# Attention scores from stacked queries and two stacked key parts: two 512-column matmuls a head and block, context keys laid first

## The chip, the core and the metric

The kernel runs on one core of a Trainium2 chip. The metric is the device time of one execution in microseconds (us); lower is better. The engines are named as in the profile: PE is TensorE's matmul stream, PEld its weight loads, DVE is VectorE, ACT ScalarE, POOL GpSimd, and SP the engine whose queue issues the DMAs.

## The reference

Two layers of a block with 512 latent tokens and 256 context tokens, each layer an input projection to three groups of heads, an output projection and a gated feed-forward. The change lies in one of the three groups, neighbourhood attention with six heads of 64 features. Its scores are

```python
s_loc = jnp.einsum('bhrqd,bhrakd->bhrqak', qg, kb) * scale + bias
s_loc = jnp.where(col_ok[:, None, :], s_loc, -jnp.inf)
s_ctx = jnp.einsum('bhrqd,bnhd->bhrqn', qg, kc) * scale
s = jnp.concatenate([s_loc.reshape(B, H, R, GRID_W, n_loc), s_ctx], axis=-1)
p = jax.nn.softmax(s, axis=-1)
o = local probabilities @ vb + context probabilities @ vc
```

A latent query sees a window of latent keys with a learned bias, and all 256 context keys, in one softmax. In the first layer the context tokens also attend to themselves; in the second layer only latent queries are left.

## The kernel before

Every float32 operand is held as two float32r parts, high and low, and a product is the sum of high by high, low by high and high by low in PSUM. So most of the kernel is `mm3` (three matmuls).

The attention takes the heads in three pairs (`Heads(pr)`, pr = 0 to 2), and a pair in blocks of 128 queries: b = 0 to 2 are three columns of the latent grid, each with 256 latent keys of its window; b = 3 collects the two borders, whose 256 keys are the first and the last tile of the latent keys; b = 4, in the first layer only, is the 256 context queries against the 256 context keys. A latent block has 512 scores a query, 256 local and 256 of the context. One head and block fill one PSUM bank, tag `a`, of which there are three.

`features_of_heads` transposes queries and keys of a pair to feature-major tiles `qt` and `kt` ([128, 2, columns]: the two heads on partitions 0 to 63 and 64 to 127, the two parts in the middle). `stack` then copies by DMA: per head a tile `st` with both parts of the queries on 128 partitions, and one with the high part of the keys twice, so that a single matmul over 128 partitions gives (high q + low q) by high k. The remaining product, high q by low k, is a matmul over 64 partitions straight from `qt` and `kt`. `product` emits this: two matmuls for 256 scores, four a head for a latent block. Pair 0 has no stacks in its first two blocks and uses `mm3` over 64 partitions, six matmuls a head.

The order on PE is written by hand (`manual_schedule`); the other engines' queues come from a scheduler. For unit n of (pair, block), PE does

1. the scores of unit n, both heads;
2. the eight transposes of unit n-1's probabilities `p` into two banks of tag `b`;
3. a filling of about 2.3 us of the output projection of the other branches (`wo`: rows `m<-u,whl`, each weight tile from a DMA `raw<-in_woa` and split by ACT and DVE into `whl`);
4. one step of the next pair's `features_of_heads` (`next(pairs[pr + 1].prepare)`);
5. the values of unit n-1 (`y<-pT,vn`), for which ACT and DVE have copied the transposes to `pT`.

Between 1 and 2 of the next unit lies the softmax: DVE adds the bias and takes the maximum (`s`, `mx`), POOL negates it (`nm`), ACT exponentiates (`p`), DVE divides (`rcl`, `p`).

`qt` and `kt` of an odd pair are in another pool than those of an even one, so the tiles of two pairs exist side by side. Each stack has two buffers.

Of the kernel before, what the change touches and what calls it, by code (L numbers as in the profile page):

```python
"""Two layers of the FNet / neighbourhood attention / GLA block with a context prefix, on one core.

The residual streams stay feature-major on chip. Dense products run on the tensor engine with
both operands split exactly into two float32r parts (x = hi + lo); the three products that count
at float32 accuracy are accumulated in PSUM.
"""
# [28 lines left out]
# ------------------------------------------------------------------ host: layout and constants  # L35
# [43 lines left out]
def _rpb_index():  # L79
    """Per tile variant: index of the bias for (query in tile, key in window), -1 where masked."""  # L80
# [60 lines left out]
# ------------------------------------------------------------------ the kernel  # L141

def hybrid_kernel(tc, d, out, dbg=None):
# [55 lines left out]
    # ---- constants  # L199
# [12 lines left out]
    # ---- residual streams  # L212
# [12 lines left out]
    # ---- conditioning vectors  # L225
# [14 lines left out]
    # ---- work that is emitted some units of dense work after what it depends on  # L240
# [18 lines left out]
    def ada_steps(l, qs, rawp, bufs, PS, nk=4, pool_streams=(1,), on_pe=()):  # L259
        """Modulation of layer l, in steps of one weight chunk; each step loads the next chunk first.  # L260

        The products are added over the feature tiles elementwise, and over the partitions by the tensor engine.
        """
# [65 lines left out]
    def ada_first(n, rawp, bufs):  # L329
        """The first layer's shift and scale (of the first norm) for one tile of features, in two steps."""  # L330
# [25 lines left out]
    def norm_add(acc, x, k, tp, e):  # L356
        """Adds the squares of one group of features."""
        if k == 0:
            act(acc, x, AF.Square)
            return  # L360
        sq = mk(tp, [128, TL], F32, "nsq", 2)[:, :x.shape[-1]]
        act(sq, x, AF.Square)
        tt(e, acc, acc, sq, ALU.add)

    def norm_acc(xs, n, tp, e):
        """Squares summed over the features of a partition."""
        acc = mk(tp, [128, TL], F32, "nacc", 2)[:, :n]
        for k in range(KD):
            norm_add(acc, xs[k], k, tp, e)
        return acc, n  # L370
# [4 lines left out]
    def norm_sums(parts, tp, more=None):  # L375
        """1 / rms of each token, with the tokens on the partitions."""
# [13 lines left out]
    def norm_spread(sums, tp):  # L390
        """1 / rms of each token (column), on every partition, in PSUM."""
# [8 lines left out]
    def norm_mod(items, tp):  # L400
        """h = rms_norm(x) * sc + sh for groups of features, written as two float32r parts.

        Without rb the columns of x are normalised already.
        """
# [26 lines left out]
    def wload(p, src, shape, rb=2, hb=2, cap=None, tag="whl", e=V):  # L431
        """A weight chunk from DRAM, as its two float32r parts."""
# [11 lines left out]
    for l in range(DEPTH):  # L444
# [6 lines left out]
        # ================= input projection, with the chunk states of the linear attention  # L451
# [27 lines left out]
        def first_projection():  # L479
            """The first column group of the first layer, as its modulation arrives by feature tiles."""  # L480
# [75 lines left out]
        def group(src, cols, specs, evac, together=0, w=None, ps=None, after=None):  # L556
            """Token-major products of one column group; specs lists (tile, first column).

            The last `together` tiles are accumulated side by side, as their operands arrive.
            """  # L560
# [63 lines left out]
        # gates, decays and the state that each chunk of 64 tokens adds, per direction  # L624
# [103 lines left out]
        def open_outputs():  # L728
            """Takes the place of the tiles of the steps above, and runs the states through the chunks."""
# [69 lines left out]
        def between():  # L799
            """After each tile of the last groups: the outputs of the linear attention, a tile at a time."""  # L800
# [13 lines left out]
        # Fourier branch, feature-major  # L814
# [38 lines left out]
        # ================= gated linear attention: outputs  # L853
# [31 lines left out]
        def stack(p, pr, t, is_q):  # L885
            """Per head both parts of the queries on 128 partitions, or the high part of the keys twice."""
            n = t.shape[-1]
            for hh in range(2):
                u = stacks[pr, hh, is_q] = mk(p, [128, n], F32R, f"st{hh}{int(is_q)}", 2)
                for part in range(2):  # L890
                    nc.sync.dma_start(out=u[64 * part:64 * part + 64].bitcast(F32),
                                      in_=t[64 * hh:64 * hh + 64, part * is_q].bitcast(F32))

        def features_of_heads(p, pr, out, sp=None):
            """Queries and keys of two heads, feature-major, as two float32r parts, in steps."""
# [4 lines left out]
            for src, dst, gain in ((kn, kt, None), (qn, qt, qg)):  # L900
                for (j0, nj) in ((0, 4), (4, 2)):
                    if src is qn and j0 and not ctx_q:
                        continue
                    sl = slice(128 * j0, 128 * (j0 + nj))
# [14 lines left out]
        def wout(src, nk, streams, kinds, whole=False, split_at=KD, begin=0):  # L919
            """Adds the projection of nk feature tiles.  # L920

            From output tile split_at on, one stream is finished before the next; with `whole` all weights stay.
            All but the last feature tile of the first `begin` output tiles of the first stream are added at once.
            """
# [43 lines left out]
        def to_features(i):  # L968
            """The heads' outputs of one tile of tokens, feature-major, as two float32r parts."""
# [7 lines left out]
        # Fourier mixing  # L977
# [5 lines left out]
        def fourier():  # L983
# [9 lines left out]
            def features(t, parts, rows):  # L993
                """The 64-point transforms and the linear map, of up to 128 (folded) positions."""
# [66 lines left out]
        def load_bias(p, h):  # L1061
            bias[h] = bi = mk(p, [128, 3, 256], F32, "bias", 2)
            nc.sync.dma_start(out=bi[:, 0:2], in_=d["rpb"][l, h])
# [339 lines left out]
```

## Time and profile before

| | |
|---|---|
| time, median of 3 runs | 1725.89 us (1725.5 to 1730.17) |
| profiled execution, first to last instruction | 1724.6 us |
| PE busy | 1680.6 us (97%), 9992 matmuls |
| DVE, ACT, POOL busy | 926.9, 584.2, 239.9 us |
| attention units, first layer | about 302 to 418 us of the span |
| attention units, second layer | about 1240 to 1334 us |
| mean granted clock of TensorE | 0.989 of full speed |

The profiled execution has no time of its own beside its span; the span lies 1.3 us below the median of the runs, and sums below are made against the span. Busy time of PE contains the modelled tail of each matmul and overlaps the weight loads, so 97% does not say that nothing could be shorter: what a group of matmuls costs is the distance from its first start to the start of what follows.

### The profile page before, as it was taken

To read this page: it belongs to the slowest core of one execution; us is meant where nothing else is said; L and a number is where in the kernel's file an instruction comes from. 1 tells how busy PE (TensorE), PEld (TensorE's weight loads), DVE (VectorE), ACT (ScalarE), POOL (GpSimd) and SP (SyncE) were. 2 spreads that over 40 slices of the span, in tenths; PEclk is the share of its full clock that TensorE was granted. 3 is DMA by queue.
4 is the path that set the end of the run, shared out by engine and by line. 5 is a ranking of instruction groups with operands and counts; after the bars stand their busy time and mean duration, and the time that the engine had idled before them with its cause. 6 is when DMAs were issued, how large, how long until landed. Compare 5 with 4: busy or idle time off the path is not lost.

```text
span 1724.6 us, 25165 instructions
## 1 busy us (share of the span) xinstructions
PE 1680.6 (97%) x9992; PEld 1433.0 (83%) x9992; DVE 926.9 (54%) x1649; ACT 584.2 (34%) x1027; POOL 239.9 (14%) x280
## 2 busy tenths in 40 slices
PE   6999999999899999999999999999899899999999
PEld 5888898777788888888888889899777888888887
DVE  6799765665855544544533434453566744344332
ACT  4474224444343422221122323831444432222220
POOL 0242331002222210000000011332100400000000
PEclk9999999899899999999999999999999999999999
DMA  9555435622233343433411311222643233323321
GB/s 323 170 163 166 157 96 167 187 57 81 75 110 111 122 147 110 137 124 106 147 62 55 122 37 38 83 88 65 190 134 93 76 122 98 98 90 93 102 86 58
DMA packets 79474, 195.94 MB, mean 114 GB/s; under 512 B 10296, under 2 KB 26492, under 8 KB 78332
## 3 DMA queue, kind: packets, MB, share of 16 engines
q1 hardware_dynamic: 79356, 194.34, 36.1%
q8 instruction: 78, 1.28, 0.3%
q14 instruction: 40, 0.33, 0.1%
HBM read 172.81 MB, written 12.85 MB: 108 GB/s over the span
## 4 chain that ended last, share of the span: by engine, by line
PE 90%; DMA 3%; DVE 2%; ACT 2%; issue 1%; SPq 0%; POOL 0%; DVEq 0%; ACTq 0%
PE a L179 32%; PE m L179 25%; PE b L179 21%; PE y L179 11%; PE b L1168 2%; DMA raw<-in_woa 1%; DVE u L190 1%; DVE whl L187 1%; DVE nacc L187 0%; DMA u<-xs 0%; DMA bias<-in_rpb 0%; ACT whl L193 0%; DMA adaw<-in_ada 0%; ACT ab L193 0%; DMA qn<-scr_q 0%
## 5 line engine op out<-in xcount | busy, mean ns | idle before, releaser
L193 ACT ACTIVATE whl<-raw 128x1024 fp32r<-128x1024 f32 (+7 forms) x222 | 204.9, 927 | 396.5 <-PE a L179 142.7
L187 DVE TENSOR_TENSOR whl<-raw,whl 128x1024 fp32r<-128x1024 f32 (+7 forms) x201 | 222.6, 1110 | 86.0 <-ACT whl L193 85.6
L179 PE MATMUL m<-u,whl 128*128 128x512 f32 (+1 forms) x1278 | 266.1, 360 | 0.4 <-DVE whl L187 0.4
L179 PE MATMUL a<-u,whl 128*128 128x512 f32 (+1 forms) x1299 | 248.1, 347 | 3.1 <-ACT u L193 2.4
L179 PEld LDWEIGHTS m<-u,whl 128*128 128x128 f32 x1278 | 213.7, 193 | 34.1 <-issue 1.2
L179 PEld LDWEIGHTS a<-u,whl 128*128 128x128 f32 x1299 | 210.0, 190 | 34.7 <-ACT u L193 2.8
L179 PE MATMUL b<-u,whl 128*128 128x512 f32 (+1 forms) x915 | 184.7, 352 | 3.7 <-DVE whl L187 2.1
L179 PEld LDWEIGHTS b<-u,whl 128*128 128x128 f32 x915 | 151.7, 192 | 28.9 <-DVE whl L187 2.6
L190 DVE SCALAR_TENSOR_TENSOR adac<-adaw,u,adac 128x512 f32<-128x512 f32 x196 | 157.4, 826 | 23.0 <-DMA adaw<-in_adaw 21.6
L179 PE MATMUL b<-whl,u 128*128 128x384 f32 (+1 forms) x696 | 143.9, 343 | 1.6 <-DVE u L190 0.9
L179 PE MATMUL m<-whl,u 128*128 128x384 f32 (+2 forms) x672 | 138.7, 343 | 0.9 <-ACT u L193 0.9
L179 PEld LDWEIGHTS b<-whl,u 128*128 128x128 f32 x696 | 121.8, 188 | 8.8 <-issue 4.7
L179 PE MATMUL a<-g,whl 128*128 128x512 f32 (+1 forms) x594 | 126.7, 370 | 0.0
L179 PEld LDWEIGHTS m<-whl,u 128*128 128x128 f32 x672 | 115.7, 188 | 11.8 <-issue 7.8
L179 PEld LDWEIGHTS a<-g,whl 128*128 128x128 f32 x594 | 103.9, 189 | 19.4 <-DVE adac L293 0.8
L190 DVE SCALAR_TENSOR_TENSOR ft<-ft,a 128x512 f32<-128x512 f32 (+1 forms) x53 | 30.5, 576 | 111.6 <-ACT ft L193 77.1
L179 PE MATMUL y<-u,whl 128*128 128x512 f32 (+1 forms) x420 | 82.5, 349 | 0.1
L179 PEld LDWEIGHTS y<-u,whl 128*128 128x128 f32 x420 | 68.1, 189 | 12.1 <-issue 0.8
L179 PE MATMUL m<-g,whl 128*128 128x512 f32 (+1 forms) x396 | 77.8, 350 | 0.0
L187 POOL TENSOR_TENSOR nacc<-nacc,nsq 128x256 f32<-128x256 f32 (+1 forms) x21 | 20.5, 975 | 395.1 <-ACT nsq L193 394.8
L179 PEld LDWEIGHTS m<-g,whl 128*128 128x128 f32 x396 | 64.7, 189 | 9.7
L179 PE MATMUL b<-g,whl 128*128 128x256 f32 (+1 forms) x396 | 72.6, 336 | 0.0
(207 smaller groups left out, 2082.2 us busy)
## 6 DMA issues: line engine op xcount, KB each, us to landing
raw<-in_w SPq DMA_DIRECT2D x104, 512.0 KB
adaw<-in_adaw SPq DMA_DIRECT2D x48, 512.0 KB
adaw<-in_adaw SPq DMA_DIRECT2D x64, 256.0 KB
raw<-in_wg SPq DMA_DIRECT2D x40, 384.0 KB
raw<-in_w SPq DMA_DIRECT2D x32, 448.0 KB
adaw<-in_ada SPq DMA_DIRECT2D x8, 1024.0 KB
raw<-in_woa SPq DMA_DIRECT2D x16, 320.0 KB
st<-kt SPq DMA_DIRECT2D x24, 192.0 KB
```

Of the source, the lines that this page charges most:

```text
L179: T.matmul(o, lhsT=l, rhs=r, start=start, stop=stop, skip_group_check=True)
L187: e.tensor_tensor(out=o, in0=a, in1=b, op=op)
L190: V.scalar_tensor_tensor(out=o, in0=a, scalar=s, in1=b, op0=op0, op1=op1)
L193: S.activation(out=o, in_=i, func=f, **kw)
L1168: T.transpose(ps[:, 128 * j:128 * j + 128], p[:, 128 * j:128 * j + 128], ident)
```

## The change

Keys are laid with the 256 context columns first. The low part of the keys is stacked twice as well (`stack` now makes kinds 0 and 1 of the keys and 2 of the queries), so the second product also runs over 128 partitions and adds low by low. A block's local and context keys are addressed as one operand of 512 columns. `products` emits per head two matmuls of 512 columns for b = 0 to 2; for b = 3 two of 384 and two of 128; for b = 4 four of 256. Pair 0's first two blocks keep 64 partitions, with three matmuls of 512 columns a head, the two heads in turns. The `qt` and `kt` of all pairs share one buffer, so the steps of the next pair wait for block 1: no step at b = 0, two at b = 1. The bias tile and the order of the value products follow the new layout of the keys.

```diff
         def stack(p, pr, t, is_q):
             n = t.shape[-1]
             for hh in range(2):
-                u = stacks[pr, hh, is_q] = mk(p, [128, n], F32R, f"st{hh}{int(is_q)}", 2)
-                for part in range(2):
-                    nc.sync.dma_start(out=u[64 * part:64 * part + 64].bitcast(F32),
-                                      in_=t[64 * hh:64 * hh + 64, part * is_q].bitcast(F32))
+                for kind in ((2,) if is_q else (0, 1)):
+                    u = stacks[pr, hh, kind] = mk(p, [128, n], F32R, f"st{hh}{kind}", 2)
+                    for part in range(2):
+                        nc.sync.dma_start(out=u[64 * part:64 * part + 64].bitcast(F32),
+                                          in_=t[64 * hh:64 * hh + 64, part if is_q else kind].bitcast(F32))
...
-                    sl = slice(128 * j0, 128 * (j0 + nj))
+                    c0 = 128 * j0 if src is qn else (128 * j0 + 256) % 768
+                    sl = slice(c0, c0 + 128 * nj)
...
-            nc.sync.dma_start(out=bi[:, 0:2], in_=d["rpb"][l, h])
-            G.memset(bi[:, 2], 0.0)
+            nc.sync.dma_start(out=bi[:, 1:3], in_=d["rpb"][l, h])
+            G.memset(bi[:, 0], 0.0)
...
-                    self.prepare = features_of_heads(own, pr, feats, np_)
+                    self.prepare = features_of_heads(nap, pr, feats, np_)
...
-            def product(self, b, o, hh, q0, k, start, stop):
-                r, q = slice(64 * hh, 64 * hh + 64), slice(q0, q0 + 128)
+            def products(self, b, parts):
                 qt, kt = feats[self.pr]
+                sps = [PA() for _ in self.hds]
                 if self.pr or b >= 2:
-                    mm(o, stacks[self.pr, hh, True][:, q], k(stacks[self.pr, hh, False]), start, False)
-                    mm(o, qt[r, 0, q], k(kt[r, 1]), False, stop)
+                    for hh, sp in enumerate(sps):
+                        st_ = [stacks[self.pr, hh, i] for i in range(3)]
+                        for n, (o, q0, k) in enumerate(parts):
+                            for i in range(2):
+                                mm(o(sp), st_[2][:, q0:q0 + 128], k(st_[i]), n == i == 0, i == 1)
+                    return sps
+                for n, (o, q0, k) in enumerate(parts):
+                    for i, j in ((0, 0), (1, 0), (0, 1)):
+                        for hh, sp in enumerate(sps):
+                            r = slice(64 * hh, 64 * hh + 64)
+                            mm(o(sp), qt[r, i, q0:q0 + 128], k(kt[r, j]), n == i == j == 0, j == 1)
+                return sps
...
+            def scores(self, b):
+                if b == 4:
+                    parts = [(lambda a, t=t: a[:, 256 * t:256 * t + 256], 512 + 128 * t, lambda k: k[:, 0:256])
+                             for t in range(2)]
+                elif b == 3:
+                    parts = [(lambda a: a[:, 0:384], 384, lambda k: k[:, 0:384]),
+                             (lambda a: a[:, 384:512], 384, lambda k: k[:, 640:768])]
                 else:
-                    mm3(o, qt[r, 0, q], qt[r, 1, q], k(kt[r, 0]), k(kt[r, 1]), start, stop)
+                    cut = ((512, 256, 1), (768, 384, 1), (768, 256, 2))[b]
+                    pair = lambda k: k[:, :cut[0]].rearrange("p (a b) -> p a b", b=cut[1])[:, ::cut[2], 0:256]
+                    parts = [(lambda a: a.rearrange("p (a b) -> p a b", a=2), 128 * b, pair)]
...
                 if pr < 2 and n < len(units):
-                    next(pairs[pr + 1].prepare, None)
+                    for _ in range((0, 2, 1, 1, 1)[b]):
+                        next(pairs[pr + 1].prepare, None)
```

On PE, at pair 0, block 2 of the first layer, the first unit that uses stacks (`st` tiles; `a` is the bank of a head), there stood before

```order
L179 MATMUL a_3550<-st_691_3392,st_693_3398 128x256
L179 MATMUL a_3550<-kt_3123,qt_3122 128x256
L179 MATMUL a_3550<-st_691_3392,st_693_3398 128x256
L179 MATMUL a_3550<-kt_3123,qt_3122 128x256
L179 MATMUL a_3566<-st_692_3395,st_694_3401 128x256
L179 MATMUL a_3566<-kt_3123,qt_3122 128x256
L179 MATMUL a_3566<-st_692_3395,st_694_3401 128x256
L179 MATMUL a_3566<-kt_3123,qt_3122 128x256
```

and now, between the same values of the unit before and the same transposes, stand

```order
L179 MATMUL a_3544<-st_691_3392,st_695_3404 128x512
L179 MATMUL a_3544<-st_692_3395,st_695_3404 128x512
L179 MATMUL a_3545<-st_693_3398,st_696_3407 128x512
L179 MATMUL a_3545<-st_694_3401,st_696_3407 128x512
```

The eight matmuls that took 128 and 64 partitions in turns are four over 128 partitions.

On SP's queue, at the start of the first layer's attention, between the loads of the residual and the bias of pair 1, there stood before (x2: one DMA for each half of the partitions)

```order
L419 DMA raw_3673<-in_woa 128x640
L891 DMA st_691_3392<-kt_3123 64x768 x2
L891 DMA st_692_3395<-kt_3123 64x768 x2
L891 DMA st_693_3398<-qt_3122 64x768 x2
L891 DMA st_694_3401<-qt_3122 64x768 x2
L1063 DMA bias_3442<-in_rpb 128x512
```

and now

```order
L419 DMA raw_3669<-in_woa 128x640
L892 DMA st_691_3392<-kt_3123 64x768 x2
L892 DMA st_692_3395<-kt_3123 64x768 x2
L892 DMA st_693_3398<-kt_3123 64x768 x2
L892 DMA st_694_3401<-kt_3123 64x768 x2
L892 DMA st_695_3404<-qt_3122 64x768 x2
L892 DMA st_696_3407<-qt_3122 64x768 x2
L1065 DMA bias_3442<-in_rpb 128x512
```

Four more DMAs stand ahead of those of the queries, and of all that follows. It is the same at the start of the second layer's attention, where two biases and the next weight tile `raw_11718<-in_woa` follow, and at each later pair.

On ACT, at the start of the second layer's attention, the split of that weight tile stood before both the rest of the keys and the softmax of block 2:

```order
L193 ACTIVATE p_11735,sml_11736<-s_11731,nm_11733 128x512
L193 ACTIVATE whl_11757<-raw_11755 128x640
L193 ACTIVATE kt_11697<-b_11773 128x256
L193 ACTIVATE p_11797,sml_11798<-s_11793,nm_11795 128x512
L193 ACTIVATE pT_11831<-b_11826 128x512
```

Now there stands

```order
L193 ACTIVATE p_11698,sml_11699<-s_11694,nm_11696 128x512
L193 ACTIVATE kt_11737<-b_11738 128x512
L193 ACTIVATE kt_11737<-b_11745 128x256
L193 ACTIVATE whl_11720<-raw_11718 128x640
L193 ACTIVATE p_11770,sml_11771<-s_11766,nm_11768 128x512
```

The keys of the next pair went ahead of the split; the softmax of block 2 still stands behind it. After the attention the order of every engine is what it was.

## Rows read from the trace of the kernel before

**Rows 1.** The page's first part: busy time, share of the span, instructions.

```profile
PE 1680.6 (97%) x9992; PEld 1433.0 (83%) x9992; DVE 926.9 (54%) x1649; ACT 584.2 (34%) x1027; POOL 239.9 (14%) x280
```

**Rows 2.** The page's chain that ended last, shares of the span by engine.

```profile
PE 90%; DMA 3%; DVE 2%; ACT 2%; issue 1%; SPq 0%; POOL 0%; DVEq 0%; ACTq 0%
```

**Rows 3.** Timeline of PE, one unit of the second layer: start, duration, what ran.

```profile
1302.54 0.38 PE L179 MATMUL a<-st,st 128*128 128x256 f32 x1
...
1305.04 1.09 PE L1168 MATMUL b<-u,p 128*128 128x128 f32 x8
1305.89 2.99 PE L179 MATMUL m<-u,whl 128*128 128x512 f32 x12
...
1309.84 0.39 PE L179 MATMUL a<-st,st 128*128 128x256 f32 x1
```

**Rows 4.** Tile `st`: its weight loads (min/median/max ns), and what waited for its DMAs.

```profile
L179 PEld LDWEIGHTS a<-st,st x92: 186/186/187, 317.6 to 1325.6; 128*128 128x128 f32 x92
...
  DMA st<-qt: 0.6, 1
```

**Rows 5.** Timeline of PE where 128 partitions follow 128 partitions: 384, 256, 512 columns.

```profile
1139.63 4.32 PE L179 MATMUL m<-whl,u 128*128 128x384 f32 x24
1143.79 4.32 PE L179 MATMUL b<-whl,u 128*128 128x384 f32 x24
...
1344.27 1.24 PE L179 MATMUL m<-u,whlw 128*128 128x256 f32 x9
...
1394.19 5.60 PE L179 MATMUL a<-u,whl 128*128 128x512 f32 x24
1399.63 5.60 PE L179 MATMUL y<-u,whl 128*128 128x512 f32 x24
```

**Rows 6.** Timeline of PE and SP, start of the first layer's attention.

```profile
302.49 0.38 PE L179 MATMUL a<-kt,qt 64*128 64x256 f32 x1 [1.56 <-ACT qt L193]
304.08 1.52 PE L179 MATMUL a<-kt,qt 64*128 64x256 f32 x11 [1.21 <-DVE qt L190]
...
305.28 3.74 SPq L891 DMA_DIRECT2D st<-kt  x4
309.14 3.46 SPq L891 DMA_DIRECT2D st<-qt  x4
```

**Rows 7.** Chain that ended last, first layer, pair 0's block 2: start, duration, what.

```profile
317.62 1.25 PE a L179 x4
...
319.33 1.29 PE a L179 x4
320.62 1.02 PE b L1168 x8
```

**Rows 8.** Windows: length, busy time of PE, PEld, DVE, ACT, POOL, clock, DMA share, GB/s.

```profile
312.60:319.30 6.70, 6.27 (x39) 5.01 (x39) 1.20 (x3) 0.38 (x1) 0.00 (x0) 0.82 1.04 287
1252.40:1258.70 6.30, 6.30 (x36) 4.50 (x34) 0.81 (x3) 0.14 (x3) 0.00 (x0) 0.90 0.72 226
306.30:316.40 10.10, 9.47 (x45) 8.15 (x43) 5.77 (x17) 4.23 (x10) 1.44 (x5) 0.57 1.04 287
1261.90:1265.30 3.40, 3.40 (x12) 2.68 (x12) 2.86 (x7) 2.34 (x6) 0.21 (x1) 0.70 0.97 245
1267.00:1326.30 59.30, 59.30 (x361) 43.13 (x359) 39.44 (x96) 25.69 (x58) 4.01 (x18) 1.00 0.31 85
```

**Rows 9.** Chain that ended last, start of the second layer's attention.

```profile
1253.98 4.68 DMA raw<-in_woa
...
1258.68 0.75 ACT whl L193
...
1261.78 3.78 PE m L179 x12
```

**Rows 10.** Timeline of DVE, second layer, the unit whose scores start at 1309.84.

```profile
1311.30 0.69 DVE L1132 CUSTOM_DVE_ANT_1 s<-a,bias 128x512 f32<-128x512 f32 x1 [2.65 <-PE a L179]
...
1317.19 0.48 DVE L1143 TENSOR_SCALAR p<-p,rcl 128x512 f32<-128x512 f32 x1
```

More of the change, by code (lines that the diff above doesn't have):

```diff
@@ L1111, in product @@
                 if self.pr or b >= 2:
-                    mm(o, stacks[self.pr, hh, True][:, q], k(stacks[self.pr, hh, False]), start, False)
-                    mm(o, qt[r, 0, q], k(kt[r, 1]), False, stop)
-                else:
-                    mm3(o, qt[r, 0, q], qt[r, 1, q], k(kt[r, 0]), k(kt[r, 1]), start, stop)
-            def scores(self, b):
-                for h in self.hds:
-                    (self.local if b < 4 else self.context)(b, h)
-            def local(self, b, h):
-                sp = PA()
-                if b < 3:
-                    loc = lambda k: k[:, 128 * b:128 * b + 256]
-                else:
-                    loc = lambda k: k[:, 0:512].rearrange("p (a b) -> p a b", a=4)[:, 0::3]
-                self.product(b, sp[:, 0:256], h % 2, 128 * b, loc, True, True)
-                self.product(b, sp[:, 256:512], h % 2, 128 * b, lambda k: k[:, 512:768], False, True)
+                    for hh, sp in enumerate(sps):
[3 more added lines that the diff above has]
+                                mm(o(sp), st_[2][:, q0:q0 + 128], k(st_[i]), n == i == 0, i == 1)
@@ new lines, in products @@
+                    return sps
[12 more added lines that the diff above has]
+                             (lambda a: a[:, 384:512], 384, lambda k: k[:, 640:768])]
+                else:
+                    cut = ((512, 256, 1), (768, 384, 1), (768, 256, 2))[b]
+                    pair = lambda k: k[:, :cut[0]].rearrange("p (a b) -> p a b", b=cut[1])[:, ::cut[2], 0:256]
+                    parts = [(lambda a: a.rearrange("p (a b) -> p a b", a=2), 128 * b, pair)]
+                for h, sp in zip(self.hds, self.products(b, parts)):
+                    (self.local if b < 4 else self.context)(b, h, sp)
@@ L1129, in local @@
+            def local(self, b, h, sp):
                 mx = mk(np_, [128, 1], F32, "mx", 4)
                 s = mk(np_, [128, 512], F32, "s", 2)
-                v = 0 if b < 3 else 1
+                v = 1 if b < 3 else 2
                 V.tensor_tensor_reduce(out=s.rearrange("p (a b) -> p a b", a=2),
                                        in0=sp.rearrange("p (a b) -> p a b", a=2),
-                                       in1=bias[h][:, v::2 - v][:, 0:2], op0=ALU.add, op1=ALU.max,
+                                       in1=bias[h][:, 0:v + 1:v], op0=ALU.add, op1=ALU.max,
@@ L1143, in local, with context @@
                 V.tensor_scalar(out=p, in0=p, scalar1=rc, scalar2=None, op0=ALU.mult)
-            def context(self, b, h):
-                sp = PA()
-                for t in range(2):
-                    self.product(b, sp[:, 256 * t:256 * t + 256], h % 2, 512 + 128 * t, lambda k: k[:, 512:768],
-                                 t == 0, True)
+            def context(self, b, h, sp):
                 s3 = sp.rearrange("p (a b) -> p a b", a=2)
@@ L1190, in values @@
                 yps = yl_[pr]
-                blks = ((b, b + 1) if b < 3 else (0, 3)) + (4, 5)
+                blks = (4, 5) + ((b, b + 1) if b < 3 else (0, 3))
                 for kt in range(4):
```

## Prediction

> **What bounds the kernel now.** I read the page's busy times first: PE is busy 97% of the span, DVE 54%, ACT 34% [rows 1]. The chain that ended last is PE for 90% of the span, and the DMAs for 3% [rows 2]. So a saving on PE is a saving of time, as long as nothing else is late where it falls. The next view is PE's timeline over one unit of the attention. There the scores of a pair and block, eight matmuls of 256 columns, take from 1302.54 to 1305.04, which is 2.50 us or 0.313 us each [rows 3]. Elsewhere, where every matmul takes 128 partitions, nine of 256 columns take 1.24 us with the tail of the last, at most 0.138 us each; 24 of 384 take 4.16 us (1139.63 to 1143.79), 0.173 each; 24 of 512 take 5.44 us (1394.19 to 1399.63), 0.227 each [rows 5]. The score matmuls are thus more than twice as dear as their columns. They take 128 and 64 partitions in turns, and 0.186 us of weight load [rows 4] plus the 0.12 us or so of 256 columns is just the 0.313 us: here the load is not hidden behind the matmul before it. That is the reading on which the forecast rests.
>
> The two starts look different. In the first layer, SP issues four DMAs of the key stacks at 305.28 and four of the query stacks from 309.14 [rows 6], with the DMA engines full: 287 GB/s, share 1.04 [rows 8]. PE begins the first stacked unit at 317.62 and stops for the second head's query stack until 319.33 [rows 7]; it is the only wait for a stack in the whole execution [rows 4]. In the second layer the chain goes through the DMA of a weight tile, which lands at 1253.98 + 4.68 = 1258.66, and its split on ACT [rows 9].
>
> **The change part by part.** *Scores from stacks.* The price before is 2.50 us a unit. For b = 0 to 2 it becomes four matmuls of 512 columns, 4 x 0.227 = 0.91, and the first load stays open, since the values before it use another shape of the array: 0.19. That is 1.10. The transposes behind them take 0.85 us from first start to the next (1305.04 to 1305.89), and keep it or lose up to 0.19 of it, as their first load can now hide. So a unit gains between 1.40 and 1.59; I take 1.45. For b = 3, four of 384 and four of 128 columns: 4 x 0.173 + 4 x 0.106 (a transpose has 128 columns: 0.85 / 8) + 0.19 = 1.31, a gain of 1.2, with the transposes 1.25. For b = 4, eight of 256: 8 x 0.138 = 1.10, or 0.9 were the tail taken off, + 0.19; I take a gain of 1.3. The units behind the starts are, in the first layer, b = 3 and 4 of pair 0 and all ten of pairs 1 and 2; in the second, b = 3 of pair 0 and all eight of pairs 1 and 2. That is 12 units at 1.45, six at 1.25 and three at 1.3: 17.4 + 7.5 + 3.9 = **28.8 us**. If a matmul of 512 columns over two pieces of the keys does not stream at 0.227 but pays its load openly (0.186 + 0.227 = 0.41), the unit gains 2.50 - 1.65 = 0.85 and the other kinds nothing: 10 us. These are the two ends.
>
> The Trainium skill gives about 131 ns for a matmul of 512 columns in a steady stream of loads and matmuls (TensorE: Matmul & The Clock Gate, section Back-to-back issue gap). The trace has 227 in such a stream. By the page's figure the 12 units would gain 12 x 4 x 0.096 = 4.6 us more; the trace decides, and the sum stays.
>
> *Pair 0's first two blocks* stay at 64 partitions with half as many matmuls. Whatever they gain is spent before the stacks have landed, so I count nothing; without that cover it would be about 1 us a unit, four units.
>
> *Four more DMAs a pair.* Each key stack now has a second tile: 4 x 192 KB (196.6 kB), 0.79 MB a pair, six pairs. Behind pairs 1 and 2 the DMA engines are at 0.31 [rows 8] and this is hidden. At the starts it isn't.
>
> First layer: the new DMAs stand ahead of the query stacks. At 287 GB/s they take 2.7 us, so the second head's stack lands at 322.0 instead of 319.3. Its two matmuls take 0.45, and the transposes start at 322.5 instead of 320.62 [rows 7]: a **loss of 1.9**. On PE the transposes of block 1, a filling and the values wait behind these scores; on DVE and ACT the softmax of block 2.
>
> Second layer: the weight tile lands 0.79 MB / 226 GB/s = 3.5 us later, at 1262.1. The scheduler moved the pair's keys ahead of it on ACT, but the softmax of block 2 still queues behind it. ACT's part of the split takes 0.75 [rows 9], DVE's about as long, so PE has the tile at 1263.7. Nine of the filling's twelve matmuls use it: 9 x 0.227 = 2.0, done at 1265.7 at the upper clock or 1267.8 at the lower, where before the filling ended at 1261.78 + 3.78 = 1265.56. A loss of 0.2 to 2.2; I take **1.2**.
>
> *The clock.* In the first layer PE stood for 1.56 and 1.21 us [rows 6], and from 306.3 to 316.4 the granted clock averages 0.57, which is nearly all at the lower level of 1.2 GHz; at 1261.9 to 1265.3 it is again 0.70 [rows 8]. The new waits, some 4.5 us around 317 to 322 and about 3 around 1261, are as long as those. Work of 10 us at half speed loses 5; nothing is the other end. I take **2.5 and 1.2**. The skill's table of the same page (section Why this matters for your kernels) warns of gaps between bursts of matmuls as what brings the lower clock, and that speaks against this change; the two windows agree with it.
>
> *Shared `qt` and `kt`, and the moved steps.* Pair 1's keys must now wait for pair 0's block 1 and the stack DMAs; PE issues the two steps at b = 1 in one go, six transposes into the two `b` banks, which the eight transposes of the unit also use. The bank of the second step comes free with the copy of the second head's transposes, which lie 2.3 us of filling earlier, so the steps themselves should not wait; the next unit's transposes wait for the splits of the keys on ACT and DVE, with the values and the scores of 1.0 and 1.1 us between as cover. From 0 to 1 us at each of four places: **1.2** in all. The layout of bias and values costs nothing: as many instructions as before.
>
> Sum: 28.8 - 1.9 - 1.2 - 2.5 - 1.2 - 1.2 = 20.8 us off the span of 1724.6, so 1703.8; the median of the runs stood 1.3 above that span: **1705 us**.
>
> **The rivals.** *(a) The starts cost next to nothing*, because the first layer's PE reaches the stacks later than I think or the lower clock does not come back. For it speaks that the clock there was already low until 316.4. Gain 26 to 31: about 1697.
>
> *(b) The softmax becomes the wait.* In the second layer DVE is busy 39.44 of 59.3 us [rows 8], about 4.9 a unit of 7.3; in a unit of 5.8 that is 85%. The unit whose scores start at 1309.84 has its second head's `p` ready at 1317.67, 7.8 us after [rows 10]. The first head's scores will be ready after two matmuls and 0.64 us instead of four and 1.25, so 7.2; PE wants it at 5.8 + 1.1 + 0.4 = 7.3. That is level, in a unit with much weight splitting besides. Against it speaks that PE never waited in these 59 us (59.30 busy). If half of the 21 units wait 0.8 us, the gain is 12: 1713.
>
> *(c) Slower: the clock stays down.* If those small waits come in every unit and hold the clock at 1.2 GHz, a unit of 5.8 us takes up to 11 where it took 7.3: 3.7 lost instead of 1.4 gained, a difference of 5.1. The gain of 21 is gone after four such units; nine, one layer's, give 1705 + 9 x 5.1 = 1751. Against it: the clock recovered within 10 us each time although the attention went on.
>
> *(d) The change does not do what it says*: the loads stay open also among matmuls over 128 partitions. 10 us of gain against 8 of losses: 1724. Against it speak the streams of rows 5.
>
> **How the numbers follow.** My forecast (gain 15 to 26) has a chance of 0.52, (a) 0.20, (b) 0.20, (d) 0.04, (c) 0.04. Its own range is 1700 to 1711. The range for 8 in 10 takes in (a) and most of (b): 1696 to 1716. A measurement of this kernel can tell 0.3%, about 5 us; (a), (b) and the forecast are all faster than that: faster 0.92, same 0.05, slower 0.03.
>
> **What the profile will show.** Score matmuls `a<-st,st` of 512 columns starting 0.23 us apart, and 1.1 us from the first to the transposes; were they 0.4 apart, (d) is right. A wait for `st<-qt` of several us at the first layer's pair 0, block 2, and one for `whl` in the second layer around 1261 to 1264, with a lower clock behind both; if they are missing, (a). Units of 5.7 to 6.6 us from scores to scores without idle time of PE; idle time ended by DVE `p` would be (b). DVE's and ACT's busy time as before. The prediction is wrong if PE waits for weight tiles or stacks also at pairs 1 and 2, which the order of SP does not suggest.

## The result, and the profile after

The changed kernel takes 1705.58 us (median of four runs, 1704.09 to 1706.62; before, beside it, 1728.03): 0.9875 of the time before, 95% interval 0.9861 to 0.9889. The forecast was 1705. The profiled execution of the changed kernel spans 1704.8 us, 19.8 less than the one before.

The page of the kernel after, busy times and the shares of the chain that ended last, beside [rows 1, 2]:

```profile
PE 1648.2 (97%) x9912; PEld 1416.3 (83%) x9912; DVE 924.1 (54%) x1649; ACT 582.3 (34%) x1027; POOL 241.4 (14%) x280
...
PE 87%; DMA 6%; DVE 3%; ACT 2%; issue 1%; SPq 1%; POOL 0%; ACTq 0%; DVEq 0%; POOLq 0%
```

PE has 32 us less to do and DVE and ACT as much as before, but the DMAs' share of the chain has doubled: some of what the matmuls gave went into waiting for transfers. PE's timeline shows both (start, duration, operation; in brackets the idle time ahead and what ended it):

```profile
305.89 0.80 PE L179 MATMUL a<-kt,qt 64*128 64x512 f32 x2 [4.69 <-ACT qt L193]
...
322.65 1.19 PE L179 MATMUL a<-st,st 128*128 128x512 f32 x2 [4.14 <-DMA st<-qt]
324.60 1.19 PE L179 MATMUL a<-st,st 128*128 128x512 f32 x2 [0.75 <-DMA bias<-in_rpb]
325.58 1.91 PE L1179 MATMUL b<-u,p 128*128 128x128 f32 x8
...
350.75 1.19 PE L179 MATMUL a<-st,st 128*128 128x512 f32 x4
351.78 1.03 PE L1179 MATMUL b<-u,p 128*128 128x128 f32 x8
352.57 1.64 PE L179 MATMUL m<-u,whl 128*128 128x512 f32 x6
...
1244.01 0.70 PE L179 MATMUL a<-st,st 128*128 128x512 f32 x2 [2.45 <-DMA st<-qt]
...
1262.36 1.92 PE L179 MATMUL a<-st,st 128*128 128x512 f32 x4 [3.53 <-DMA st<-qt]
...
1287.96 1.16 PE L179 MATMUL a<-st,st 128*128 128x512 f32 x4 [0.94 <-DMA st<-qt]
```

The unit at 350.75 is what [rows 3] showed before. From its first score to the transposes it takes 1.03 us instead of 2.50, and from there to the filling 0.79 instead of 0.85: 1.82 where it was 3.35. This distance, first score to filling, is called the cost of a unit below. It is 2.02 for b = 3 and 1.85 for b = 4. The other rows are the price. At 324.60 the second head's matmuls wait once more; the profile names a bias there, whose DMAs stand right behind the query stacks on SP, though these matmuls read stacks alone. The tile view of `st` in the kernel after, against [rows 4] (first what issued the stacks, then who waited for whom):

```profile
L892 SPq DMA_DIRECT2D st<-kt x48: 461/564/1604, 308.6 to 1280.9; - x48
...
  DMA st<-qt: 18.8, 7
...
  ACT kt L193: 13.7, 2
  PE a L179: 11.1, 4
```

Before, 0.6 us in one place was all that was waited for a stack; now PE's matmuls alone wait four times, 11.1 us. SP's timeline of the kernel after, beside [rows 6], shows what comes late:

```profile
308.56 7.21 SPq L892 DMA_DIRECT2D st<-kt  x8
315.85 3.82 SPq L892 DMA_DIRECT2D st<-qt  x4
...
1244.24 6.31 SPq L892 DMA_DIRECT2D st<-kt  x8
...
1253.28 2.39 SPq L892 DMA_DIRECT2D st<-qt  x4
```

Eight DMAs of keys keep SP for 7.21 us, where four took 3.74. The query stacks, which stand behind them, start at 315.85 instead of 309.14; 3.3 us of this is that the key stacks themselves began later (308.56 instead of 305.28). And the windows of the kernel after (busy time of the engines, then the granted clock, the DMA engines' share, GB/s), beside [rows 8]:

```profile
322.00:332.00 10.00, 8.60 (x35) 6.64 (x37) 5.05 (x13) 3.10 (x8) 0.41 (x2) 0.57 0.98 276
...
1264.00:1267.50 3.50, 3.50 (x17) 3.14 (x16) 2.30 (x8) 2.12 (x5) 0.42 (x2) 0.73 0.03 12
345.00:405.00 60.00, 59.95 (x459) 50.45 (x460) 45.62 (x119) 29.09 (x75) 3.33 (x16) 1.00 0.26 64
...
430.00:480.00 50.00, 45.94 (x263) 39.30 (x262) 38.79 (x69) 21.75 (x38) 14.73 (x13) 1.00 0.19 61
```

From 322 to 332, behind the wait of 4.14 us, the clock averages 0.57 of full speed, mostly its lower level of 1.2 GHz. In the 60 us from 345 on PE has no gap to speak of. From 1264 to 1267.5, behind the wait of 3.53 us, the clock is at 0.73.

Where the time went is a sum of stretches between three marks of each layer, read from PE's timelines. Negative is gained; the second column is another execution of the same changed kernel (the first experiment), 1704.4 us long.

| stretch | after | repeat | what the cheaper units alone would give |
|---|---|---|---|
| to the first score, layer 1 | +3.4 | +3.1 | 0 |
| from there to pair 0, b = 3 | +4.0 | +3.4 | 0 |
| from there to pair 2, b = 4 | -15.8 | -16.1 | -16.2 |
| from there to the first score, layer 2 | -5.3 | -1.0 | -1.5 |
| from there to pair 0, b = 3 | +0.3 | +2.4 | 0 |
| from there to pair 2, b = 3 | -5.6 | -10.2 | -11.8 |
| from there to the end | -0.7 | -1.7 | -1.3 |
| sum | -19.8 | -20.2 | -30.8 |

### The profile page after: what moved, and what is told of

It is laid out like the page before. It is cut to its first block, busy times and chain, and to the rows that moved or that the text cites. A ratio compares the mean times of both kernels' runs of the same rounds, so it can differ in the third digit from the quotient of the medians.

```text
span 1704.8 us, 25072 instructions
## 1 busy us (share of the span) xinstructions
PE 1648.2 (97%) x9912; PEld 1416.3 (83%) x9912; DVE 924.1 (54%) x1649; ACT 582.3 (34%) x1027; POOL 241.4 (14%) x280
## 4 chain that ended last, share of the span: by engine, by line
PE 87%; DMA 6%; DVE 3%; ACT 2%; issue 1%; SPq 1%; POOL 0%; ACTq 0%; DVEq 0%; POOLq 0%
PE a L179 30%; PE m L179 24%; PE b L179 20%; PE y L179 11%; PE b L1179 1%; DMA vn<-scr_v 1%; DVE u L190 1%; DMA st<-kt 1%; DVE whl L187 1%; DMA st<-qt 1%; DMA u<-in_xt 1%; DVE nacc L187 1%; DMA u<-xs 1%; DMA u<-in_cxt 0%; DMA qn<-scr_q 0%
```

## The experiments

The theory was that before, each change between matmuls over 128 and over 64 partitions left a weight load open, and that the change gained by having none among a unit's scores. Rivals: that there were twice as many matmuls, or that they were short. A second theory, on what was lost: the four more DMAs a pair; its rival: the shared `qt` and `kt`. In the code, `...` stands for lines left out. This table holds what PE's timelines of all kernels show (the cost of a unit as above, and the way from a layer's first score to the scores of pair 0, b = 3); the times are medians, the ratios are to the kernel before on the same chip.

| kernel | unit cost b = 0 to 2 / 3 / 4 | first score to pair 0, b = 3: layer 1, layer 2 | time, ratio [95%] |
|---|---|---|---|
| before | 3.35 / 3.35 / 3.35 | 22.6, 26.4 | 1 |
| after | 1.82 / 2.02 / 1.85 | 26.6, 26.6 | 1705.58, 0.9875 [0.9861, 0.9889] |
| 1 repeat | 1.82 / 2.02 / 1.85 | 26.0, 28.7 | 1705.88, 0.9888 [0.9871, 0.9904] |
| 2 grouped | 1.95 / 1.95 / 1.95 | 22.1, 21.4 | 1695.93, 0.9826 [0.9800, 0.9851] |
| 3 halves of 256 | 1.85 / 2.01 / 1.85 | 25.8, 24.6 | 1707.14, 0.9896 [0.9875, 0.9918] |
| 4 grouped, 512 columns | 1.95 / 2.00 / 1.95 | 20.4, 23.5 | 1698.07, 0.9837 [0.9819, 0.9855] |
| 5 in turns, 512 columns | 2.56 / 3.35 / 3.35 | 24.5, 22.5 | 1717.51, 0.9949 [0.9933, 0.9964] |
| 6 no stacks | 1.75 / 1.85 / 1.75 | 17.1, 19.9 | 1688.61, 0.9787 [0.9769, 0.9804] |
| 7 heads apart | 1.75 / 2.31 / 2.10 | 21.0, 21.6 | 1694.14, 0.9819 [0.9802, 0.9836] |
| 8 DMAs alone | 3.35 / 3.35 / 3.35 | 24.0, 26.9 | 1731.46, 1.0026 [1.0013, 1.0039] |
| 9 grouped 512 and DMAs | 1.95 / 2.00 / 1.95 | 24.3, 24.9 | 1702.11, 0.9868 [0.9845, 0.9891] |
| 10 own buffers, layer 2 | 1.82 / 2.01 / 1.85 | 27.2, 25.7 | 1704.23, 0.9864 [0.9844, 0.9883] |

**1. The change once more**, without an edit.

> The changed kernel once more, unaltered. Two things in its first profile lie outside the change: the attention of the first layer began 3.4 us late (a DMA of a weight tile landed late), and the feed-forward behind it ran 4 us faster than before, because a stretch at the lower clock was missing. If these are chance of one execution, the repeat shows other values for both, and the total stays at 1704 to 1708. If they belong to the change, both come back.

The time is the same. The late first score came back (3.1 us), the faster stretch behind the first layer did not (1.0 us gained, where the units alone give 1.5). What is waited for at the start of the second layer differs too; PE's timeline of this execution:

```profile
1246.41 1.26 PE L179 MATMUL a<-st,st 128*128 128x512 f32 x4 [1.15 <-DMA st<-qt]
1253.13 4.12 PE L179 MATMUL m<-u,whl 128*128 128x512 f32 x9 [3.88 <-ACT whl L193]
...
1264.18 1.17 PE L179 MATMUL a<-st,st 128*128 128x512 f32 x4 [0.21 <-DMA st<-qt]
...
1288.55 1.16 PE L179 MATMUL a<-st,st 128*128 128x512 f32 x4 [1.31 <-DMA st<-qt]
```

Here it is the weight tile that is 3.88 us late, and pair 1's stacks 0.21; in the first execution pair 1's stacks were 3.53 us late and the weight tile cost PE less than 1 us. Which of the DMAs is late differs between executions of one kernel.

**2. The kernel before with its scores grouped**: its own stacks, DMAs, 256-column matmuls and layout, both heads' matmuls over 128 partitions first and then both heads' over 64.

```diff
-for h in self.hds: (self.local if b < 4 else self.context)(b, h)
...
+for hh, sp in enumerate(sps):
+    for n, (c, q0, k) in enumerate(parts):
+        mm(sp[:, c:c + 256], stacks[self.pr, hh, True][:, q0:q0 + 128], k(stacks[self.pr, hh, False]), n == 0, False)
+for hh, sp in enumerate(sps):
...
+    for n, (c, q0, k) in enumerate(parts):
+        mm(sp[:, c:c + 256], qt[r, 0, q0:q0 + 128], k(kt[r, 1]), False, True)
```

> The kernel before with one edit: the eight score matmuls of a unit keep their form (256 columns, low keys over 64 partitions, no further DMAs) but come as four over 128 partitions and then four over 64. Theory (the weight load lies open at each change between 128 and 64 partitions): two changes a unit instead of eight, 0.19 + 4 x 0.12 + 0.19 + 4 x 0.12 = 1.3 instead of 2.5 us, 23 units, so 22 to 27 us faster than before: 1700 to 1706. Rival (the gain of the change came from half as many and twice as long matmuls): no difference, 1726 to 1729.

PE's timeline of one unit:

```profile
344.64 0.74 PE L179 MATMUL a<-st,st 128*128 128x256 f32 x4
345.30 0.51 PE L179 MATMUL a<-kt,qt 64*128 64x256 f32 x4
345.74 1.09 PE L1184 MATMUL b<-u,p 128*128 128x128 f32 x8
346.59 2.31 PE L179 MATMUL m<-u,whl 128*128 128x512 f32 x9
```

The same eight matmuls of 256 columns take 1.10 us to the transposes instead of 2.50. Only their order differs, so it was the order and not their number or length. It is 0.2 us less than expected (1.3): the four matmuls over 64 partitions, two of each head, take 0.44 us (345.30 to 345.74), which leaves about 0.25 behind a load of 0.19, the time of two such streams and not of four. So by an estimate from these rows some 1.2 of the 1.40 us are the switches, and 0.2 are two heads' matmuls side by side (experiments 4 and 6). This kernel is faster than the change, with nothing of its stacks and layout.

**3. The change with its 512-column matmuls cut in two.**

```diff
+if b < 3:
+    for j in range(2):
+        mm(sp[:, 256 * j:256 * j + 256], st_[2][:, q0:q0 + 128], k(st_[i])[:, j], i == j == 0, i == 1)
+    continue
```

> The changed kernel with each 512-column score matmul cut into two of 256 columns, all still over 128 partitions, stacks and DMAs as in the change. Theory: 8 x 0.12 + 0.19 = 1.15 us for the scores of a unit against 1.1, so 0 to 3 us slower than the changed kernel: 1705 to 1709. Rival (number and length of the matmuls): 14 units go back to 2.5 us, about 20 us slower: 1725.

A unit of eight matmuls of 256 columns costs 1.85 us, one of four of 512 columns 1.82. The number and length of the matmuls are worth 0.03 us; that rival falls.

**4. Context keys first, 512 columns, but the low keys over 64 partitions and grouped**, so that neither the second key stack nor shared buffers are needed; steps as before.

```diff
-for kind in ((2,) if is_q else (0, 1)):
+for kind in ((2,) if is_q else (0,)):
...
-            for i in range(2):
-                mm(o(sp), st_[2][:, q0:q0 + 128], k(st_[i]), n == i == 0, i == 1)
+            mm(o(sp), stacks[self.pr, hh, 2][:, q0:q0 + 128], k(stacks[self.pr, hh, 0]), n == 0, False)
+    for n, (o, q0, k) in enumerate(parts):
+        for hh, sp in enumerate(sps):
...
+            mm(o(sp), qt[r, 0, q0:q0 + 128], k(kt[r, 1]), False, True)
...
```

> The changed kernel without the stacked low keys: the layout with the context keys first and 512 columns stay, the low keys are taken over 64 partitions from the unstacked tile, grouped behind the two matmuls over 128 partitions; tiles of the pairs, steps and number of DMAs as in the kernel before. Theory: 0.19 + 2 x 0.227 + 0.19 + 2 x 0.227 = 1.3 us a unit, a gain of 1.2 to 1.4 in 23 units, without the DMA losses at the starts and the waits for stacks in the second layer: 1696 to 1702, faster than the changed kernel by 3 to 9. If the two heads' matmuls over 64 partitions also run side by side, 0.2 less a unit. Rival (the DMAs cost nothing, the stacked low keys are what gains): 1706 to 1715.

Its units of b = 0 to 2 cost 0.13 us more than the change's and it is still some 8 us faster (0.9837 against 0.9875 and 0.9888). So the change lost elsewhere more than its second stack won. PE's timeline of a unit shows something else:

```profile
345.35 0.73 PE L179 MATMUL a<-st,st 128*128 128x512 f32 x2
346.02 0.50 PE L179 MATMUL a<-kt,qt 64*128 64x512 f32 x2
346.45 1.09 PE L1181 MATMUL b<-u,p 128*128 128x128 f32 x8
```

Two matmuls of 512 columns over 64 partitions, one on each half, are done 0.43 us after the first started, 0.19 of which an open load would be. The two over 128 partitions take 0.67. That leaves about 0.24 us for two streams that take 0.227 each elsewhere [rows 5].

**5. The same, in turns**: 128, 64, 128, 64 partitions (the edit against the fourth).

```diff
 for hh, sp in enumerate(sps):
     for n, (o, q0, k) in enumerate(parts):
         mm(o(sp), stacks[self.pr, hh, 2][:, q0:q0 + 128], k(stacks[self.pr, hh, 0]), n == 0, False)
-for n, (o, q0, k) in enumerate(parts):
-    for hh, sp in enumerate(sps):
         mm(o(sp), qt[r, 0, q0:q0 + 128], k(kt[r, 1]), False, True)
```

> The fourth experiment's 512-column matmuls over 128 and 64 partitions, not grouped but in turns, a head at a time. If each switch between 128 and 64 partitions leaves a weight load of 0.186 us open whatever the length of the matmul, a unit of four takes 4 x (0.186 + 0.227) = 1.65 us from the first score to the transposes instead of the 1.1 of the grouped order, one of block 3 about 2.6 instead of 1.2 and one of block 4 about 2.5 instead of 1.1: 12 x 0.54 + 6 x 1.4 + 3 x 1.4 = 19 us lost, about 1717. Rival: not the switch but the number of matmuls or the length of the weight stream was dear: 1698 as in the grouped order.

PE's timeline:

```profile
350.39 0.51 PE L179 MATMUL a<-st,st 128*128 128x512 f32 x1
350.83 0.49 PE L179 MATMUL a<-kt,qt 64*128 64x512 f32 x1
351.25 0.50 PE L179 MATMUL a<-st,st 128*128 128x512 f32 x1
351.68 0.49 PE L179 MATMUL a<-kt,qt 64*128 64x512 f32 x1
352.11 1.09 PE L1179 MATMUL b<-u,p 128*128 128x128 f32 x8
```

Each starts 0.43 us after the one ahead: 0.24 of stream and 0.19 of load. Four take 1.72 (1.65 expected), and the 384 + 128 and 256-column units are back at 3.35. The time, 1717.5, is the one expected. The price of a switch is thus measured from both sides: some 0.2 us each, by grouping and by taking the groups apart. The Trainium skill (TensorEngine Tiling (Array Packing), section Key Properties) says that a change of the tiling mode drains the engine, and that different tiles may load and multiply in parallel. The traces agree with the first, and put 0.19 us on it; whether that time is the drain or the open load, whose record is 0.186 us long, they do not tell. Experiment 6 agrees with the second.

**6. No stacks at all**: the fourth kernel with all three products over 64 partitions, the heads in turns, and no stack DMA.

```diff
-    stack(np_, 0, feats[0][i], i == 0)
...
-if self.pr or b >= 2:
...
 for n, (o, q0, k) in enumerate(parts):
     for i, j in ((0, 0), (1, 0), (0, 1)):
         for hh, sp in enumerate(sps):
             mm(o(sp), qt[r, i, q0:q0 + 128], k(kt[r, j]), n == i == j == 0, j == 1)
```

> The fourth experiment's kernel without any stacks: all three products of a head over 64 partitions, the two heads in turns, and none of the eight stack DMAs a pair. In the fourth experiment's trace two 64-partition matmuls of 512 columns, one a head, lie 0.44 us ahead of the transposes, 0.19 of which is the open load: they stream side by side. If that is so, a unit takes 3 x 0.23 + 0.19 us of scores instead of 1.1, 0.2 us less in 21 units, and the waits for stacks (3.8 us) and their DMAs go: 1686 to 1693, faster than all the others. Rival: matmuls of two heads over 64 partitions stream one after the other: 6 x 0.227 + 0.19 = 1.55 us a unit, 9 us more than the fourth experiment's, 4 back from the waits: about 1703.

PE's timeline:

```profile
322.45 1.07 PE L179 MATMUL a<-kt,qt 64*128 64x384 f32 x12
323.46 1.13 PE L1158 MATMUL b<-u,p 128*128 128x128 f32 x8
...
345.78 0.96 PE L179 MATMUL a<-kt,qt 64*128 64x512 f32 x6
346.67 1.11 PE L1158 MATMUL b<-u,p 128*128 128x128 f32 x8
347.54 3.42 PE L179 MATMUL m<-u,whl 128*128 128x256 f32 x21
```

Six matmuls of 512 columns take 0.89 us: three times 0.23 for a pair of heads, and 0.19. The two halves do stream side by side: the three products of both heads pass in three streams, where the change needs four, and its twelve stack DMAs a pair (eight in the kernel before) bought nothing. The way from the first score to b = 3 is also the shortest of all, 17.1 us in the first layer against the change's 26.6. At 1688.6 us (1684.42 to 1691.94) this kernel beats both.

**7. As the sixth, one head after the other.**

```diff
-for n, (o, q0, k) in enumerate(parts):
-    for i, j in ((0, 0), (1, 0), (0, 1)):
-        for hh, sp in enumerate(sps):
+for hh, sp in enumerate(sps):
+    for n, (o, q0, k) in enumerate(parts):
+        for i, j in ((0, 0), (1, 0), (0, 1)):
```

> As the kernel without stacks, but a head's three products after each other, then the other head's. If matmuls on the two halves of the partitions stream side by side only when they alternate, this doubles the scores: 0.68 us more in 16 units, 0.84 in six and 0.7 in three, about 18 us slower than the kernel without stacks. Rival: 64-partition matmuls are cheap by themselves, or the hardware looks further ahead: no difference.

Neither was right. PE's timeline:

```profile
324.44 1.53 PE L179 MATMUL a<-kt,qt 64*128 64x384 f32 x12
325.90 1.09 PE L1158 MATMUL b<-u,p 128*128 128x128 f32 x8
...
348.50 0.97 PE L179 MATMUL a<-kt,qt 64*128 64x512 f32 x6
349.40 1.24 PE L1158 MATMUL b<-u,p 128*128 128x128 f32 x8
```

With three matmuls of a head in a row the two heads still run side by side (0.90 us); with six in a row only in part (1.46 us for b = 3, where turns take 1.01). The units explain 6 x 0.46 + 3 x 0.35 = 3.8 of the 5.5 us.

**8. The kernel before with the DMAs of the change alone**: four more a pair, of the same size and in the same place, to device memory that nobody reads (those of the change go to SBUF).

```diff
+if not is_q:
+    x = mk(drp, [128, n], F32, f"sx{l}{pr}{hh}")
+    for part in range(2):
+        nc.sync.dma_start(out=x[64 * part:64 * part + 64], in_=t[64 * hh:64 * hh + 64, 1].bitcast(F32))
```

> The kernel before, with the four more DMAs a pair alone: the low keys go, 192 KB a DMA, into memory that nobody reads, ahead of the query stacks as in the change. My theory is that the starts of both layers pay for these DMAs, as the forecast had it (1.9 and 1.2 us of waiting and up to 3.7 us of lower clock): 3 to 8 us slower than before, with longer waits for st<-qt at pair 0, block 2. Rival: the DMAs are hidden and what the change loses at pair 1 and 2 comes from the shared buffers: no change, within 2 us.

It is 0.26% slower, 4.5 us (2.2 to 6.7). The DMAs are not hidden, as the theory had it. The longer waits for `st<-qt` that the theory named are not in this trace, though. In it the two starts are 1.4 and 0.6 us longer; in the second PE waits for the weight tile, the wait that the forecast had put there for the change:

```profile
1266.38 0.50 PE L179 MATMUL m<-u,whl 128*128 128x512 f32 x1 [2.07 <-ACT whl L193]
```

Of the 5 us by which this profiled execution is longer, 2.3 lie ahead of the first score and 1.2 between the layers, where nothing was added. So the price rests on the medians, and the trace shows only part of it.

**9. The fourth kernel with the same four DMAs a pair** (the edit of the eighth).

> The fourth experiment's kernel (low keys over 64 partitions, own buffers) plus four DMAs a pair of the size of the change's second key stack, into memory that nobody reads. If the DMAs are what the change loses against that kernel, it goes from 1698 to 1703 to 1707. Rival: the loss comes from the shared buffers and the moved steps, and this stays within 2 us of 1698.

0.9868 against 0.9837 is 5 us, the lower end of what was expected, though the two intervals overlap. The starts show it: 24.3 and 24.9 us where the fourth kernel had 20.4 and 23.5, 5.3 us in sum, with these waits in the first layer on PE's timeline:

```profile
319.53 0.47 PE L179 MATMUL a<-st,st 128*128 128x512 f32 x1 [2.05 <-DMA st<-qt]
321.40 0.77 PE L179 MATMUL a<-st,st 128*128 128x512 f32 x1 [1.40 <-DMA bias<-in_rpb]
```

**10. The change with own buffers for pair 1 in the second layer**, and one step a block there (four small tiles have two buffers instead of four there, to make room).

```diff
-self.prepare = features_of_heads(nap, pr, feats, np_)
+self.prepare = features_of_heads(nap if ctx_q else own, pr, feats, np_)
...
-for _ in range((0, 2, 1, 1, 1)[b]):
+for _ in range((0, 2, 1, 1, 1)[b] if ctx_q else 1):
```

> The change with buffers of their own for the queries and keys of pair 1 in the second layer, and one step a block there as before (four small tiles get two buffers instead of four to make room). If the shared buffers delay the second layer's stacks, ACT no longer waits 5 to 8 us for the stack DMAs before it writes kt, PE no longer waits for st<-qt at pair 1, block 0, and the kernel is 2 to 5 us faster than the change: 1701 to 1704. Rival: the eight DMAs of key stacks a pair are late whichever buffer they read: no change, 1705 to 1706, with the same waits.

ACT's first copy into `kt` for pair 1, in the kernel after and here:

```profile
1243.34 0.87 ACT L193 ACTIVATE kt<-b 128x512 fp32r<-128x512 f32 x2 [7.58 <-DMA st<-kt]
```

```profile
1245.01 0.38 ACT L193 ACTIVATE kt<-b 128x256 fp32r<-128x256 f32 x1 [4.32 <-PE b L909]
```

The wait for the stack DMAs is gone, but PE's timeline here still has a wait for pair 1's stacks, of a size between those of the first two executions of the change:

```profile
1262.46 1.24 PE L179 MATMUL a<-st,st 128*128 128x512 f32 x4 [0.99 <-DMA st<-qt]
```

The time is 2 to 4 us below the change's two ratios, inside their intervals. So the shared buffer holds ACT up, but what that costs is at most a few us and was not told from nothing.

## Why the prediction was right, and which steps were not

**Units.** Forecast 28.8 us, measured 12 x 1.53 + 6 x 1.33 + 3 x 1.50 = 30.8. The mechanism, a load left open at each switch, holds (experiments 2, 3 and 5), and its size of 0.19 us too. The scores came out at 1.03 instead of 1.10: of PE's matmuls in the unit at 350.75 the second starts 0.33 us behind the first and the others 0.23 us apart, so only about 0.10 of the load at the unit's head falls into this distance. The transposes gained the small part that the forecast left open.

**First layer's start.** Forecast 1.9 + 2.5 us with the lower clock; measured 4.0 and 3.4. The wait for the query stacks and the 0.57 window behind it are where they were put, and both terms are about right. Counted from the layer's first score, the transposes of block 2 start 1.6 and 2.4 us later than before, and from there to pair 0's b = 3 another 2.4 and 1.0 are lost. The delay was worked out from bytes, 2.7 us; PE starts on the second head's stack at 324.60 instead of 319.33, which is 1.9 us more than the first score was late (2.6 in the repeat). SP's issue of the query stacks was put off by more, 3.5 us (7.21 instead of 3.74).

**Second layer's start.** Forecast 1.2 + 1.2; measured 0.3 and 2.4. The wait for `whl` of 3.88 us that was forecast is in the second execution. A wait for pair 0's query stacks was forecast for the first layer only; here it is there too, 2.45 us in the first execution and 1.15 in the second.

**Pairs 1 and 2.** This is the step that failed, although the total came out: the DMAs behind pairs 1 and 2 were called hidden, and PE was to wait there for no stack; such a wait was named as the sign that the prediction is wrong. Only the shared buffers and moved steps had a price there, "From 0 to 1 us at each of four places". In the second layer PE waits 3.53 and 0.94 us for stacks in one execution, 0.21 and 1.31 in the other. Of the 11.8 us that the units give from pair 0's b = 3 to pair 2's, 6.2 and 1.6 were lost; 4.5 of the 6.2 are the two waits, and the lower clock behind the first of them (0.73) goes with the rest. SP, PE and a window of the kernel before, and the window of the kernel after:

```profile
1266.75 2.38 SPq L891 DMA_DIRECT2D st<-qt  x4
1273.56 0.39 PE L179 MATMUL a<-st,st 128*128 128x256 f32 x1
1266.75:1273.50 6.75, 6.75 (x47) 4.80 (x43) 4.82 (x11) 2.63 (x6) 0.92 (x4) 1.00 0.70 200
```

```profile
1253.28:1262.22 8.94, 5.55 (x47) 4.49 (x43) 5.36 (x12) 2.74 (x6) 0.92 (x4) 1.00 1.07 196
```

Before, pair 1's query stacks were issued at 1266.75, 6.8 us ahead of their unit at 1273.56. After, SP issued them at 1253.28, as soon as ACT had written the queries (1253.26) and behind the eight key DMAs, and they landed at 1262.22, while PE was ready for them at 1262.36 - 3.53 = 1258.83, 5.6 us behind the issue. From issue to landing, 8.9 us, the share of the DMA engines was 1.07 on the mean, against 0.70 before; in the repeat it took 5.6 us, at 0.83. The shorter units brought the moment of need nearer, and fuller DMA engines put off the landing; the forecast had looked at neither for these pairs, only at how busy the DMA engines were on the average of the whole stretch (0.31).

**Outside the change.** The first score came 3.4 us later, behind a wait for `ACT qt` of 4.69 us where before waited 1.56 [rows 6]. PE's matmuls up to there are the same in all kernels, and their first scores lie between 302.49 and 306.17, that of the kernel before the earliest; the eighth experiment, whose work up to there is that of the kernel before, has 304.77. So this is most likely scatter, although it came back in the repeat. So is the stretch behind the first layer: 430 to 480 us ran at 1.00 of the clock in the first execution after, 0.90 in the repeat and before. In the first execution the two cancel, 3.4 lost and 3.8 gained. The total agreed with the forecast better than its parts, and that it did so within 1 us is luck: the units gave 2 us more than forecast, pairs 1 and 2 took 0.5 to 5 more, the second start in one execution 2 less, and the late first score was not forecast at all.

**The rivals.** (a) falls with the waits at the starts. (b), the softmax, is not there: in the waits of PE for the whole execution after there is this row (total, times, longest), all of it in the layers' first blocks:

```profile
PE b L1179 <- DVE p L1158: 1.3, 3, 0.6
```

(c): the clock was back at 1.00 from 345 to 405 in the first layer, and from 1267.5 to 1310 in the second. (d) falls with units of 1.82 us.

**What the loss was.** Of 30.8 us some 20 arrived. The four more DMAs a pair cost 4.5 (experiment 8) to 5 (experiment 9). The change's units are 12 x 0.13 - 6 x 0.02 + 3 x 0.10 = 1.7 us in sum cheaper than the ninth kernel's, and by the ratios it is still 1 to 3.5 us slower, with intervals that overlap. Taken as they are, the medians leave another 3 to 5 us for what only the change has: PE must wait for the second stacks themselves, the shared buffers, the doubled step. Experiment 10 does not part these; that stays open, and the remainder itself is not clear of the noise.

## What to carry to other kernels

Group matmuls by how many partitions they contract over: a switch between 64 and 128 leaves the weight load open, 0.19 us here, and reordering alone was worth 30 us, of which by the estimate in experiment 2 some 5 are two heads' matmuls side by side. Before copying operands together to fill 128 partitions, see whether two matmuls on the two halves run side by side; here they do, and the copies with their DMAs were pure cost. And do not call an added transfer hidden because the DMA engines are idle on the average: take their share between its issue and the moment at which it is needed (0.31 over the stretch of the layer before, 1.07 there after), and shorten that time by what the change itself saves.

## What was not expected of the hardware

Two streams over 64 partitions each run at the price of one also if they don't alternate: three of one half and then three of the other, 512 columns each, take 0.90 us like six in turns (0.89). With six and six of shorter ones, part of it is lost (1.46 against 1.01 us, 1.25 against 0.91). The Trainium skill (TensorEngine Tiling (Array Packing), section Theoretical Speedup) gives up to twice the speed for a small dimension of 64; experiment 6 has that in full.

SP took 7.21 us for the eight key-stack DMAs at the first layer's start, 0.9 us each, where the shortest such issue took 461 ns. In that row single issues last 0.46 to 0.86 us, and once SP waits 1.1 us for the landing of an earlier load of `u`. Full DMA engines alone don't explain it: from 1253.28, with the engines at 1.07, four query stacks were issued in 2.39 us. The cause stays open.
